# A tile's channel transform made relative to its neighbour's, and half of the four-point step given to GpSimd, in the Fourier layer of an encoder

## The chip, the cores and the metric

The kernel runs on one core of one Trainium2 chip. A core has TensorE (PE; its weight loads are shown apart, as PEld), VectorE (DVE), ScalarE (ACT), GpSimd (POOL) and SyncE (SP), and DMA queues fed by SP, ACT and POOL. The metric is the device time of one execution in microseconds. Of three runs of the kernel before, the median was 1577.85 us (1577.05 to 1578.53).

## The reference

An encoder of width 1024 with two layers is applied to two sequences, one of 2048 positions and one of 512: first windowed attention, then Fourier mixing, each behind an RMS norm, and a last RMS norm. The change is in the Fourier layer:

```python
def fourier_layer(x, g, w_gate, w_out):
    b, s, d = x.shape
    h = rmsnorm(x, g)
    hg = h.astype(jnp.float32).reshape(b, s, N_FGROUPS, FGROUP_CH)
    f = jnp.fft.fftn(hg, axes=(1, 3), norm="ortho").real
    f = f.reshape(b, s, d).astype(x.dtype)
    gate = h @ w_gate
    return x + (f * jax.nn.silu(gate)) @ w_out
```

There are four groups of 256 channels. The two-dimensional transform is a transform over the channels of each group, then one over the positions.

## The kernel before

The attention layer fills the time to about 1058 us, the Fourier layer the rest. This layer's first stage, from about 1060 to 1323 us and called the gates stage here, works on the 20 tiles of 128 positions as ten pairs. The four tiles of the short sequence are one group of four; the long sequence's tiles a, a+4, a+8 and a+12, for a of 0 to 3, are the other four. Two successive pairs are one group; gi is a group's number, n a pair's (0 to 9).

**What a pair goes through.** Its two tiles are loaded, normed (L1056, L110, L111 and the multiplication on L1081), and turned on PE (transposes, L1089). The turned tiles are then combined: F[1] to F[4] are sums and differences of the two tiles' halves (`sums`, an ACT copy on L1112 for some, and DVE on L1119), and `odd` makes one more difference in the bank (L1103). Each matrix that PE is to multiply is held as two parts, a rounded one and what the rounding left: ACT casts, DVE subtracts (`split`, L1013 and L1015; `own`, L1096 and L1097). The parts of F[i] are S[i], those of a turned tile A.

**The gate products** of a pair (`gates`) are six products of 128x512, W, Z and X being their three PSUM banks. Two pairs of tiles share multiplications in a Strassen-like scheme, so that sums of banks give the four blocks of the result: c11, c12, c22 and W itself. DVE adds on L1227 (c12 and Z), L1232 (c22 and W) and L1236 (c11 and X). After L1232 PE writes W again, with the product named N4. Each block goes through a SiLU (tanh on ACT, L1197, a scalar-tensor-tensor on DVE, L1198) into a buffer gt and by POOL's queue to memory (s2d, L1201).

**The channel transform** of the next pair's two tiles is done between these products, at the hooks. Hooks 1 to 4 turn and combine the next pair, hook 5 does its second tile, hook 6 its first:

- The second tile (`z_odd_even`, at hook 5) uses S[1] and the parts of the bank that `odd` made: an even and an odd half, 16 matmuls of 128x256. Each of four banks is taken out by an ACT copy of the odd half with a factor (L1160) and a DVE scalar-tensor-tensor that adds the even half (L1161).
- The first tile (`z`, at hook 6) multiplies its own parts A by both halves of the table in three products each (`matmul3`, L117): 24 matmuls of 128x256. Each of two banks is taken out by one ACT copy (L1139).

The results are 128x1024 buffers, zs[0] and zs[1].

**The four-point step** (`radix4`, called by `combine`, at hook 6 of every second pair) takes the four z of a group: six operations of 128x1024 on DVE (L1261). Four results go to memory by POOL's queue (L1337), except those of the last group (gi = 4), which stay on the chip. The six, with z0 to z3 for the four z:

```python
e = z0+z2; z0 = z0-z2; z2 = z1+z3; z1 = z1-z3; z3 = e-z2; e = e+z2
```

**What sets the order.** Each engine works its own queue in order, which a scheduler makes from the order of the program text; semaphores hold an instruction until what it reads is ready or what it overwrites has been read. Buffers with a fixed number of copies are taken in turn: five PSUM banks for transposes and transforms, three for W, Z and X, eight of the kind hT, sixteen for z and other 128x1024 tiles (R).

Of the kernel before, what the change touches and what calls it, by code (L numbers as in the profile page):

```python
# [10 lines left out]
F32R = mybir.dt.float32r  # L11
# [3 lines left out]
ALU = mybir.AluOpType  # L15
# [4 lines left out]
P = 128  # L20
# [22 lines left out]
def encoder(  # L43
# [3 lines left out]
    PE, ACT, DVE, POOL, SP = nc.tensor, nc.scalar, nc.vector, nc.gpsimd, nc.sync  # L47
# [18 lines left out]
    odd = dram.tile([3, 2, P, D], F32, name="odd")  # L66
# [38 lines left out]
    def htile(shape, dtype, name):  # L105
        return main.tile(shape, dtype, align_bytes=LINE, tag="hT", bufs=8, name=name)
# [884 lines left out]
    def fourier_phase(tail):  # L991
        with ExitStack() as es:
# [10 lines left out]
            def right(shape, dtype, name):  # L1003
                return zp.tile(shape, dtype, align_bytes=LINE, tag="R", bufs=16, name=name)
# [3 lines left out]
            def zt(name):  # L1008
                return right([P, D], F32, name)

            def split(t, src, lo_engine=DVE, place=lambda key, ins: ins):

                place("act", ACT.copy(t[:, 0], src))  # L1013
                for cs in (slice(0, 256), slice(256, 512)) if lo_engine is POOL else (slice(0, 512),):
                    place("dve", lo_engine.tensor_tensor(t[:, 1, cs], src[:, cs], f32(t[:, 0, cs]), ALU.subtract))  # L1015
                return t[:, 0], t[:, 1]
# [51 lines left out]
            class Pair:  # L1068
# [71 lines left out]
                        out, ps.rearrange("p (g o n) -> p g o n", g=2, o=2), AF.Copy, scale=1.0 if t >= SEQ // P else 0.5  # L1140
                    )

                def z_odd_even(self):

                    t = self.ts[1]
                    self.zs[1] = zt(f"z{t}")
                    for g in range(4):
                        ps = bank(f"z{t}_{g}")
                        for odd, m in enumerate((self.S[1], self.diff)):

                            to = ps[:, odd * 256 : odd * 256 + 256].rearrange("p (a n) -> p a n", a=2)
                            for part in range(2):
                                PE.matmul(
                                    to, m[part][:, g * P : (g + 1) * P], ch[:, 0, :, odd * P : (odd + 1) * P],
                                    start=part == 0, stop=part == 1,
                                )
                        v = ps.rearrange("p (o a n) -> p a o n", o=2, a=2)
                        out = self.zs[1][:, g * 256 : g * 256 + 256].rearrange("p (n o) -> p o n", o=2)
                        scale = 1.0 if t >= SEQ // P else 0.5
                        ACT.activation(out, v[:, 1], AF.Copy, scale=scale)  # L1160
                        last_z[0] = DVE.scalar_tensor_tensor(out, v[:, 0], scale, out, ALU.mult, ALU.add)  # L1161
# [98 lines left out]
            def tt(out, a, b, op):  # L1260
                DVE.tensor_tensor(out, a, b, op)  # L1261

            def radix4(z, name):

                e = zt(f"e{name}")
                tt(e, z[0], z[2], ALU.add)
                tt(z[0], z[0], z[2], ALU.subtract)
                tt(z[2], z[1], z[3], ALU.add)
                tt(z[1], z[1], z[3], ALU.subtract)
                tt(z[3], e, z[2], ALU.subtract)  # L1270
                tt(e, e, z[2], ALU.add)
                return e, z[3], z[0], z[1]
# [6 lines left out]
            pairs = [Pair(2 * gi + i // 2, tiles[i : i + 2]) for gi, tiles in enumerate(order) for i in (0, 2)]  # L1279
# [43 lines left out]
            def turns4(pr):  # L1323
                pr.sums(3)
                pr.parts(3)

            def combine(pr):

                if pr.n % 2 == 0:
                    return  # L1330
                gi = pr.n // 2
                r = radix4(pairs[pr.n - 1].zs + pr.zs, f"r{gi}")
                if gi == 4:
                    kept.extend(r)
                    return
                for i in range(4):
                    POOL.dma_start(gsd[i] if gi == 0 else evd[gi - 1, i] if i < 2 else odd[gi - 1, i - 2], r[i])  # L1337
# [3 lines left out]
            pr = pairs[0]  # L1341
# [16 lines left out]
            for n, pr in enumerate(pairs[:-1]):  # L1358
                nx = pairs[n + 1]
                if n:  # L1360
                    for i in range(2):
                        nx.load(1 - i)
                        nx.norms(1 - i)
                gates(pr, {
                    1: [lambda: turns1(nx)], 2: [lambda: turns2(nx)], 3: [lambda: turns3(nx)], 4: [lambda: turns4(nx)],
                    5: [lambda: nx.z_odd_even()],
                    6: [lambda: nx.z(0), lambda: nx.z(1), lambda: combine(nx)],
                })
            gfb = fp.tile([P, D], F32, tag="gb", bufs=1, name="gfb")
            SP.dma_start(gfb, bass.AP(gf.tensor, gf.offset, [[0, P], [1, D]]))  # L1370
# [386 lines left out]
            for i, l in enumerate((w0, w2)):  # L1757
                for a in range(3):
                    t = zt(f"ev{a}_{i}")
# [15 lines left out]
            e, g4r = pm(w0[0], w0[2], "e0")  # L1775
            f, g4s = pm(w0[1], w0[3], "f0")
# [16 lines left out]
            for a in range(4):  # L1793
                for i, l in enumerate((pc, qs)):
# [3 lines left out]
                    t = zt(f"od{a}_{i}")  # L1798
# [28 lines left out]
            o = Outs(6, position("p6", 6, *G[6], pair(6, 16, 0), None, p6))  # L1827
# [19 lines left out]
            for k1, k2 in ((1, 7), (7, 3), (3, 5), (5, None)):  # L1847
                name, tiles = f"p{k1}", pair(k1, 16, 0)
# [29 lines left out]
                o = nxt["o"]  # L1878
# [108 lines left out]
```

## Time and profile before

| | |
|---|---|
| median of three runs | 1577.85 us |
| the profiled execution: its time, its span | 1577.83 us, 1576.1 us |
| PE busy | 1565.2 us, 99% of the span |
| DVE busy | 1150.7 us, 73% |
| ACT busy | 878.1 us, 56% |
| POOL busy | 444.6 us, 28% |
| one pair in the gates stage (pairs 4 to 7) | 25.66 to 25.67 us |

The profile is of one execution. Its busy time counts how long an engine had an instruction under way. A row of a timeline gives the start in us from the span's beginning, the duration, the engine, the line, the operation, what it writes and reads with the shape, and how many such instructions are in the row; in brackets stands how long the engine was idle before it and what ended that. A row of the chain of waits gives a start, a duration and the work that the end of the span depended on. A row of groups gives the number of instructions, their busy time and the mean of one in ns, then the idle time ahead of them. Names such as W, Z, X, z, c and gt are those of the program; tTb and tTd are parts of turned tiles, trb the bank a transpose wrote, invb and ssb the norm's sums.

### The profile page before, as it was taken

Reading aid. Unit: us, or ns where it says so; the run is one execution under the profiler, and the core shown is the slowest. Engines: PE = TensorE matmul, PEld = TensorE weight load, DVE = VectorE, ACT = ScalarE, POOL = GpSimd, SP = SyncE. Lnnn points to the kernel's source line nnn. Section 1 sums busy time; section 2 is a strip of 40 time slices with the busy share of each in tenths; the row PEclk is TensorE's granted clock in tenths of the full one; section 3 lists DMA queues with packets and bytes.
Section 4 is the critical chain, followed back from the end, with each engine's and each line's share of the span. In section 5 each row is a group of like instructions: output and inputs, shape, how many; then the busy total and the mean of one; then the engine's idle time right before and its main releaser. Section 6 shows DMA issues by size and latency. Waiting matters only on the chain.

```text
span 1576.1 us, 27737 instructions
## 1 busy us (share of the span) xinstructions
PE 1565.2 (99%) x9882; PEld 1315.6 (83%) x9882; DVE 1150.7 (73%) x2793; ACT 878.1 (56%) x2096; POOL 444.6 (28%) x614
## 2 busy tenths in 40 slices
PE   9999999999999999999999999999999999999998
PEld 7888888888888888988888888888888888888886
DVE  6888555877548786378764577668878778989886
ACT  7788535776247684257852477646655554333353
POOL 2575642421404314024223242222111111101100
PEclk9999999999999999999999999999999999999999
DMA  8598695565856667656649656675666569557852
GB/s 296 203 332 287 223 365 210 208 247 202 297 214 214 204 248 256 242 193 235 238 170 326 232 208 208 248 253 200 210 222 233 185 219 399 193 201 267 312 195 94
DMA packets 100997, 373.90 MB, mean 237 GB/s; under 512 B 11268, under 2 KB 22284, under 8 KB 83453
## 3 DMA queue, kind: packets, MB, share of 16 engines
q1 hardware_dynamic: 83148, 298.17, 53.7%
q0 software_dynamic: 16400, 70.04, 11.5%
q10 hardware_dynamic: 1312, 3.94, 0.6%
q8 instruction: 78, 1.28, 0.3%
q14 instruction: 59, 0.48, 0.1%
HBM read 280.84 MB, written 91.26 MB: 236 GB/s over the span
## 4 chain that ended last, share of the span: by engine, by line
PE 94%; DVE 4%; issue 1%; ACT 1%; DMA 0%; POOL 0%; SPq 0%; POOLq 0%; DVEq 0%; ACTq 0%
PE gp L117 14%; PE qp L117 14%; PE spt L117 11%; PE op L117 7%; PE W L117 7%; PE av L615 6%; PE spt L530 6%; PE fo L117 5%; PE vp L117 3%; PE Z L117 3%; PE pt L589 3%; PE Wo L117 3%; PE z L117 2%; PE X L117 2%; PE Zo L117 2%; PE ABp L117 1%
## 5 line engine op out<-in xcount | busy, mean ns | idle before, releaser
L117 PE MATMUL gp<-h,wg 128*128 128x512 f32 x960 | 237.7, 396 | 0.0
L117 PE MATMUL qp<-h,wq 128*128 128x512 f32 x960 | 237.0, 396 | 0.0
L549 DVE CUSTOM_DVE_ANT_0 S<-spt,b 128x385 f32<-128x385 f32 (+1 forms) x320 | 156.5, 528 | 105.5 <-PE spt L530 68.3
L117 PEld LDWEIGHTS gp<-h,wg 128*128 128x128 f32 x960 | 174.9, 188 | 37.3 <-issue 1.0
L117 PEld LDWEIGHTS qp<-h,wq 128*128 128x128 f32 x960 | 174.9, 188 | 36.4 <-issue 0.3
L557 ACT ACTIVATE S<-S 128x385 f32<-128x385 f32 (+1 forms) x320 | 188.8, 596 | 19.5 <-DVE S L549 19.3
L597 ACT CAST pts<-pt 128x384 fp32r<-128x384 f32 (+1 forms) x240 | 100.6, 458 | 167.0 <-PE pt L589 158.2
L598 DVE TENSOR_TENSOR pts<-pt,pts 128x384 fp32r<-128x384 f32 (+1 forms) x240 | 114.3, 520 | 23.4 <-ACT pts L597 22.2
L639 POOL TENSOR_TENSOR uT<-o,uT 128x256 fp32r<-128x256 f32 x75 | 55.6, 741 | 229.5 <-ACT uT L638 229.4
L117 PE MATMUL spt<-wo,uT 128*128 128x512 f32 x480 | 120.3, 391 | 0.0
L117 PE MATMUL op<-wo,uT 128*128 128x512 f32 x480 | 118.9, 391 | 0.0
L530 PE MATMUL spt<-kwin,qab 64*128 64x384 f32 (+1 forms) x960 | 118.8, 353 | 0.0
L615 PEld LDWEIGHTS av<-pts,v 128*128 128x128 f32 x576 | 101.4, 188 | 18.8
L615 PE MATMUL av<-pts,v 128*128 128x512 f32 (+1 forms) x576 | 115.7, 341 | 0.0
L117 PE MATMUL fo<-wo,tTu 128*128 128x512 f32 x480 | 115.4, 392 | 0.0
L117 PEld LDWEIGHTS op<-wo,uT 128*128 128x128 f32 x480 | 89.4, 188 | 18.5
L117 PEld LDWEIGHTS spt<-wo,uT 128*128 128x128 f32 x480 | 89.1, 188 | 18.3
L117 PEld LDWEIGHTS fo<-wo,tTu 128*128 128x128 f32 x480 | 88.3, 188 | 17.3
L569 DVE TENSOR_SCALAR S<-S 128x384 f32<-128x384 f32 (+1 forms) x192 | 95.9, 499 | 6.8
L530 PEld LDWEIGHTS spt<-kwin,qab 64*128 64x128 f32 x960 | 74.7, 186 | 28.4 <-issue 26.4
L635 POOL TENSOR_TENSOR o<-o,s 128x256 f32<-128x256 f32 x75 | 55.4, 738 | 134.5 <-DVE o L633 134.1
L589 PEld LDWEIGHTS pt<-ident,S 64*128 64x128 f32 x1328 | 78.3, 138 | 4.2 <-issue 2.1
(331 smaller groups left out, 3173.2 us busy)
## 6 DMA issues: line engine op xcount, KB each, us to landing
wo<-wsd SPq DMA_DIRECT2D x32, 1024.0 KB, 5.0
wq<-wsd SPq DMA_DIRECT2D x31, 1024.0 KB, 7.1
wg<-wsd SPq DMA_DIRECT2D x31, 1024.0 KB, 5.8
x<-x1d SPq DMA_DIRECT2D x40, 512.0 KB, 3.9
b<-b21d SPq DMA_DIRECT2D x40, 512.0 KB, 4.8
b<-rowd SPq DMA_DIRECT2D x40, 384.0 KB, 4.3
xs<-in_x_dram SPq DMA_DIRECT2D x23, 512.0 KB, 7.5
s2d<-gt POOLq DMA_DIRECT2D x40, 256.0 KB, 5.2
```

What stands on the lines that cost most here:

```text
L117: ins = pe(PE.matmul(out, a[i], b[j], start=start and i + j == 0, stop=stop and i == 1, skip_group_check=more))
L530: pe(PE.matmul(banks[j][:, 2 + k0 * P : 2 + k1 * P], res["q"][rows, qp, b * P : (b + 1) * P], kwin[g][rows, kp, b * P + k0 * P : b * P + k ...
L549: seq(DVE, DVE.tensor_tensor_reduce(out=s[:, e0:e1], in0=ps[:, 1 + e0 : 1 + e1], in1=st["bias"][:, j, 386 - e1 : 386 - e0][:, ::-1], scale ...
L557: last_exp[0] = seq(ACT, ACT.activation(s[:, e0:e1], s[:, e0:e1], AF.Exp, bias=s[:, 386:387], scale=-1.0, accum_out=s[:, 387:388]))
L569: seq(DVE, DVE.tensor_scalar(s[:, ks], s[:, ks], den, None, ALU.mult))
L589: pe(PE.transpose(ps[h][:, kb, j, :], ss[j][rows, 1 + kb * P : 1 + (kb + 1) * P], ident[rows, rows]))
L597: seq(ACT, ACT.copy(hi, ps[:, k0:k1]))
L598: seq(DVE, DVE.tensor_tensor(lo, ps[:, k0:k1], f32(hi), ALU.subtract))
L615: pe(PE.matmul(to, v, pt, start=n == part == 0, stop=part == 1 and n in (1, len(todo) - 1), skip_group_check=n > 1,))
L635: eng.tensor_tensor(o, o, s, ALU.mult)
L639: low = eng.tensor_tensor(lo, o, f32(hi), ALU.subtract)
```

## The change

For the pairs with n of 2 or more, the first tile's transform becomes one of the same kind as the second's. `cross`, run at hook 4, replaces F[4] by 2 F[3] - F[4] (one DVE operation) and splits it into a new hT buffer (tC). At hook 6 `z_odd_even(0)` multiplies S[4] and these parts: 16 matmuls for 24, four ACT copies and four DVE operations of 128x256 for two ACT copies of 128x512. Its zs[0] holds the first tile's transform less the second's.

`radix4_relative` then takes the four-point step from such relative inputs, for gi of 1 to 4. It has six operations too. For gi of 1, 2 and 3 three of them (`slow`) go to POOL, each in four pieces of 128x256; for gi = 4 all stay on DVE. The group gi = 0 keeps the old step.

```diff
--- before.py
+++ after.py
@@ -1140,13 +1140,20 @@
                         out, ps.rearrange("p (g o n) -> p g o n", g=2, o=2), AF.Copy, scale=1.0 if t >= SEQ // P else 0.5
                     )

-                def z_odd_even(self):
-
-                    t = self.ts[1]
-                    self.zs[1] = zt(f"z{t}")
+                def cross(self):
+
+                    F3, F4 = self.F[3], self.F[4]
+                    DVE.scalar_tensor_tensor(F4, F3, 2.0, F4, ALU.mult, ALU.subtract)
+                    self.mixed = split(htile([P, 2, 512], F32R, f"tC{self.n}"), F4)
+
+                def z_odd_even(self, i=1):
+
+                    t = self.ts[i]
+                    out_of = (self.S[1], self.diff) if i else (self.S[4], self.mixed)
+                    self.zs[i] = zt(f"z{t}")
                     for g in range(4):
                         ps = bank(f"z{t}_{g}")
-                        for odd, m in enumerate((self.S[1], self.diff)):
+                        for odd, m in enumerate(out_of):

                             to = ps[:, odd * 256 : odd * 256 + 256].rearrange("p (a n) -> p a n", a=2)
                             for part in range(2):
@@ -1155,7 +1162,7 @@
                                     start=part == 0, stop=part == 1,
                                 )
                         v = ps.rearrange("p (o a n) -> p a o n", o=2, a=2)
-                        out = self.zs[1][:, g * 256 : g * 256 + 256].rearrange("p (n o) -> p o n", o=2)
+                        out = self.zs[i][:, g * 256 : g * 256 + 256].rearrange("p (n o) -> p o n", o=2)
                         scale = 1.0 if t >= SEQ // P else 0.5
                         ACT.activation(out, v[:, 1], AF.Copy, scale=scale)
                         last_z[0] = DVE.scalar_tensor_tensor(out, v[:, 0], scale, out, ALU.mult, ALU.add)
@@ -1260,6 +1267,22 @@
             def tt(out, a, b, op):
                 DVE.tensor_tensor(out, a, b, op)

+            def on_pool(out, a, b, op):
+                for i in range(4):
+                    cs = slice(i * 256, i * 256 + 256)
+                    POOL.tensor_tensor(out[:, cs], a[:, cs], b[:, cs], op)
+
+            def radix4_relative(z, name, slow=tt):
+
+                e = zt(f"e{name}")
+                tt(e, z[0], z[2], ALU.add)
+                slow(z[0], z[0], z[2], ALU.subtract)
+                tt(z[2], z[1], z[3], ALU.add)
+                slow(z[1], z[1], z[3], ALU.subtract)
+                DVE.scalar_tensor_tensor(z[2], z[2], 2.0, e, ALU.mult, ALU.add)
+                slow(z[0], z[0], z[1], ALU.add)
+                return z[2], e, z[0], z[1]
+
             def radix4(z, name):

                 e = zt(f"e{name}")
@@ -1323,13 +1346,19 @@
             def turns4(pr):
                 pr.sums(3)
                 pr.parts(3)
+                if pr.n > 1:
+                    pr.cross()

             def combine(pr):

                 if pr.n % 2 == 0:
                     return
                 gi = pr.n // 2
-                r = radix4(pairs[pr.n - 1].zs + pr.zs, f"r{gi}")
+                zs = pairs[pr.n - 1].zs + pr.zs
+                if gi:
+                    r = radix4_relative(zs, f"r{gi}", tt if gi == 4 else on_pool)
+                else:
+                    r = radix4(zs, f"r{gi}")
                 if gi == 4:
                     kept.extend(r)
                     return
@@ -1364,7 +1393,7 @@
                 gates(pr, {
                     1: [lambda: turns1(nx)], 2: [lambda: turns2(nx)], 3: [lambda: turns3(nx)], 4: [lambda: turns4(nx)],
                     5: [lambda: nx.z_odd_even()],
-                    6: [lambda: nx.z(0), lambda: nx.z(1), lambda: combine(nx)],
+                    6: [lambda: nx.z_odd_even(0) if nx.n > 1 else [nx.z(hf) for hf in range(2)], lambda: combine(nx)],
                 })
             gfb = fp.tile([P, D], F32, tag="gb", bufs=1, name="gfb")
             SP.dma_start(gfb, bass.AP(gf.tensor, gf.offset, [[0, P], [1, D]]))
```

Ahead of each part below stands the engine and the place. er is e, and a name's first number tells which tile it belongs to.

DVE at the four-point step of gi = 1, made before and during the products of pair 3. Before (z0 and z4 are zs[0] and zs[1] of the group's first pair, z8 and z12 those of its second; afterwards z0 and z8 are the relative ones):

```order
L1081 SCALAR_TENSOR_TENSOR x1_1_13651<-x1_1_13651,invb1_13656,g1b_12526 128x1024
L1261 TENSOR_TENSOR er1_13631<-z0_13354,z8_13602 128x1024
L1261 TENSOR_TENSOR z0_13354<-z0_13354,z8_13602 128x1024
L1261 TENSOR_TENSOR z8_13602<-z4_13309,z12_13557 128x1024
L1261 TENSOR_TENSOR z4_13309<-z4_13309,z12_13557 128x1024
L1261 TENSOR_TENSOR z12_13557<-er1_13631,z8_13602 128x1024
L1261 TENSOR_TENSOR er1_13631<-er1_13631,z8_13602 128x1024
L1097 TENSOR_TENSOR tTb5_1_13705<-trb5_1_13700,tTb5_1_13705 128x512
L1119 TENSOR_TENSOR s1_4_13708<-s1_4_13708,trb5_1_13700 128x512
```

After:

```order
L1168 SCALAR_TENSOR_TENSOR z8_13610<-z8_2_13625,z8_13610 128x2x128
L1168 SCALAR_TENSOR_TENSOR z8_13610<-z8_3_13632,z8_13610 128x2x128
L1081 SCALAR_TENSOR_TENSOR x1_5_13659<-x1_5_13659,invb5_13664,g1b_12526 128x1024
L1268 TENSOR_TENSOR er1_13639<-z0_13358,z8_13610 128x1024
L1081 SCALAR_TENSOR_TENSOR x1_1_13668<-x1_1_13668,invb1_13673,g1b_12526 128x1024
L1268 TENSOR_TENSOR z8_13610<-z4_13313,z12_13565 128x1024
L1282 SCALAR_TENSOR_TENSOR z8_13610<-z8_13610,er1_13639 128x1024
L1097 TENSOR_TENSOR tTb5_1_13722<-trb5_1_13717,tTb5_1_13722 128x512
L1119 TENSOR_TENSOR s1_4_13725<-s1_4_13725,trb5_1_13717 128x512
```

The six operations in a row have become three, with the two norm multiplications (L1081) now behind the evacuations and around the first of them; the next pair's first row (tTb) follows the scalar-tensor-tensor.

DVE further on in the same pair, around the addition of c and W. Before:

```order
L1227 TENSOR_TENSOR c12_3_13727<-c12_3_13727,Z3_13661 128x512
L1015 TENSOR_TENSOR S4_4_13776<-s4_4_13749,S4_4_13776 128x512
L1119 TENSOR_TENSOR s4_4_13749<-trb1_0_13729,s4_4_13749 128x512
L1198 SCALAR_TENSOR_TENSOR gt8_1_13772<-gt8_1_13772,c12_3_13727 128x512
L1232 TENSOR_TENSOR c3_13663<-c3_13663,W3_13660 128x512
L1015 TENSOR_TENSOR S3_4_13803<-s4_4_13749,S3_4_13803 128x512
```

After:

```order
L1234 TENSOR_TENSOR c12_3_13744<-c12_3_13744,Z3_13678 128x512
L1015 TENSOR_TENSOR S4_4_13793<-s4_4_13766,S4_4_13793 128x512
L1119 TENSOR_TENSOR s4_4_13766<-trb1_0_13746,s4_4_13766 128x512
L1205 SCALAR_TENSOR_TENSOR gt8_1_13789<-gt8_1_13789,c12_3_13744 128x512
L1146 SCALAR_TENSOR_TENSOR s4_4_13766<-s4_4_13766 128x512
L1239 TENSOR_TENSOR c3_13680<-c3_13680,W3_13677 128x512
L1015 TENSOR_TENSOR S3_4_13820<-s4_4_13766,S3_4_13820 128x512
L1015 TENSOR_TENSOR tC4_13824<-s4_4_13766,tC4_13824 128x512
```

The crossing (L1146 of the new text) stands between the SiLU of c12 and the addition of c and W; the new split (tC) stands behind that addition and S[3].

POOL over the same place. Before:

```order
L1201 DMA s2d0_81<-gt4_0_13598 128x512
L1337 DMA odd_83<-z0_13354 128x1024
L1337 DMA odd_83<-z4_13309 128x1024
L1337 DMA evd_113<-z12_13557 128x1024
L1337 DMA evd_113<-er1_13631 128x1024
L1201 DMA s2d0_81<-gt8_1_13772 128x512
```

After:

```order
L111 TENSOR_TENSOR invb1_13673<-invb1_13673,mhalf_77 128x1
L1273 TENSOR_TENSOR z0_13358<-z0_13358,z8_13610 128x256 x4
L1366 DMA evd_113<-er1_13639 128x1024
L1273 TENSOR_TENSOR z4_13313<-z4_13313,z12_13565 128x256 x4
L1273 TENSOR_TENSOR z0_13358<-z0_13358,z4_13313 128x256 x4
L1366 DMA evd_113<-z8_13610 128x1024
L1366 DMA odd_83<-z0_13358 128x1024
L1366 DMA odd_83<-z4_13313 128x1024
L1208 DMA s2d0_81<-gt8_1_13789 128x512
```

Three groups of four pieces now stand among the four stores, all ahead of the next gated tile's store.

## The prediction

> **What bounds the kernel now.** I read the page's totals first, then its chain, then the stage the change touches: the busy time of each engine in four successive pairs of the gates stage.
>
> ```profile
> span 1576.1 us, 27737 instructions
> PE 1565.2 (99%) x9882; PEld 1315.6 (83%) x9882; DVE 1150.7 (73%) x2793; ACT 878.1 (56%) x2096; POOL 444.6 (28%) x614
> PEclk9999999999999999999999999999999999999999
> PE 94%; DVE 4%; issue 1%; ACT 1%; DMA 0%; POOL 0%; SPq 0%; POOLq 0%; DVEq 0%; ACTq 0%
> ```
> ```profile
> 1169.52:1195.19 25.67, 25.67 (x143) 22.22 (x142) 17.05 (x29) 13.99 (x27) 4.03 (x8) 1.00 0.44 163
> 1195.19:1220.85 25.66, 25.66 (x142) 22.21 (x141) 23.31 (x34) 13.99 (x27) 4.88 (x9) 1.00 0.75 259
> 1220.85:1246.52 25.67, 25.67 (x142) 22.22 (x141) 17.36 (x30) 14.14 (x27) 4.22 (x8) 1.00 0.42 152
> ```
>
> The columns of the second fence are the stretch, its length, then PE, PEld, DVE, ACT and POOL busy, the clock and DMA. PE is busy the whole 25.67 us of every pair, at full clock (the PEclk row, and 1.00 here). So a matmul taken away shortens the pair by its own time, as long as everything else still arrives. DVE is the next engine: 17 us in a pair without a four-point step, 23.31 of 25.66 in one with it. ACT at 14 and POOL at 4 to 5 have room. Everything below is about whether DVE, given more small work, still delivers to PE in the pairs with a four-point step.
>
> **The change part by part.** *Matmuls removed.* The chain of waits between 1165 and 1225 us shows both channel transforms and what stands around them:
>
> ```profile
> 1187.82 1.91 PE z L1153 x16
> ...
> 1210.08 2.72 PE W L117 x12
> 1212.80 0.68 PE X L117 x3
> 1213.48 1.91 PE z L1153 x16
> 1215.40 2.75 PE W L117 x12
> 1218.14 2.87 PE z L117 x24
> ```
>
> The first tile's transform, 24 matmuls of 128x256 in 2.87 us, becomes 16 of the kind that now take 1.91 us for the second tile. That is 0.96 us for each of the eight pairs with n of 2 to 9: 8 x 0.96 = **-7.68 us**. No cover is needed, since PE is the bound.
>
> *DVE and ACT work added.* The mean duration of each kind of instruction in the gates stage:
>
> ```profile
> L1015 DVE TENSOR_TENSOR S<-s,S 128x512 fp32r<-128x512 f32 x40 | 27.5, 688 | 0.2
> L1013 ACT CAST S<-s 128x512 fp32r<-128x512 f32 x40 | 24.9, 623 | 32.9 <-DVE s L1119 18.1 <-PE W L117 12.2 <-PE Z L117 2.5
> L1081 DVE SCALAR_TENSOR_TENSOR x<-x,invb,g1b 128x1024 f32<-128x1024 f32 x16 | 20.5, 1279 | 8.9 <-POOL invb L111 8.9
> L1261 DVE TENSOR_TENSOR z<-z,z 128x1024 f32<-128x1024 f32 x15 | 18.4, 1225 | 0.4
> L1161 DVE SCALAR_TENSOR_TENSOR z<-z,z 128x256 f32<-128x256 f32 x40 | 14.4, 415 | 0.0
> L1139 ACT ACTIVATE z<-z 128x512 f32<-128x512 f32 x20 | 12.6, 632 | 8.3 <-PE z L117 8.2
> L1160 ACT ACTIVATE z<-z 128x256 f32<-128x256 f32 x40 | 12.6, 393 | 0.8 <-PE z L1153 0.8
> ```
>
> Per changed pair DVE gets the crossing (one 128x512 of the L1015 size, 0.69), the low half of its split (0.69) and four evacuations (4 x 0.415 = 1.66): 3.04 us. ACT gets a cast (0.62) and 4 x 0.393 for 2 x 0.632: +0.93, hidden at 14 of 25.67. In pairs without a four-point step DVE goes from 17 to 20 of 24.7 us, and it sits idle for long stretches there, ahead of the next tiles' work:
>
> ```profile
> 1224.91 1.28 DVE L1081 SCALAR_TENSOR_TENSOR x<-x,invb,g1b 128x1024 f32<-128x1024 f32 x1 [4.01 <-POOL invb L111]
> 1228.70 0.69 DVE L1097 TENSOR_TENSOR tTb<-trb,tTb 128x512 fp32r<-128x512 f32 x1 [2.50 <-ACT tTb L1096]
> ```
>
> So I cost the added work there at nothing; the cover is these 4.01 and 2.50 us. For the group of gi = 4 all six operations stay on DVE (one as a scalar-tensor-tensor of the same size), and no next pair's transposes stand behind them: nothing again.
>
> *The four-point step with pieces on GpSimd (gi = 1, 2, 3).* Three 128x1024 operations leave DVE, 3 x 1.225 = 3.68 us; twelve pieces of 128x256 come to POOL. POOL's rows for pieces of that shape, and a DVE row beside the second of them:
>
> ```profile
> 1072.63 1.43 POOL L1015 TENSOR_TENSOR wN<-w32N,wN 128x256 fp32r<-128x256 f32 x2 [12.36 <-ACT wN L1013]
> 1076.09 1.89 POOL L1015 TENSOR_TENSOR wN<-w32N,wN 128x256 fp32r<-128x256 f32 x2 [2.03 <-ACT wN L1013]
> ```
> ```profile
> 1077.30 1.23 DVE L1015 TENSOR_TENSOR wT<-w32N,wT 128x512 fp32r<-128x512 f32 x1
> ```
>
> Two pieces take 1.43 us alone, so four take 2.9, and twelve 8.7: in POOL's free 20 us, but not in parallel with DVE at will. The second pair of pieces took 1.89, +0.46, and the DVE operation between two SBUF operands beside them took 1.23 where its kind takes 0.69 (the S row): +0.54. The two hold each other up. [...]
>
> Where DVE stands in such a pair today, from 1195.19 us on (t = 0, where PE begins a pair's first product):
>
> ```profile
> 1191.66 0.41 DVE L1161 SCALAR_TENSOR_TENSOR z<-z,z 128x256 f32<-128x256 f32 x1
> ...
> 1196.06 1.23 DVE L1261 TENSOR_TENSOR er<-z,z 128x1024 f32<-128x1024 f32 x1
> 1197.32 3.75 DVE L1261 TENSOR_TENSOR z<-z,z 128x1024 f32<-128x1024 f32 x3
> ...
> 1202.35 1.22 DVE L1261 TENSOR_TENSOR er<-er,z 128x1024 f32<-128x1024 f32 x1
> 1203.50 0.69 DVE L1097 TENSOR_TENSOR tTb<-trb,tTb 128x512 fp32r<-128x512 f32 x1
> ...
> 1205.46 0.69 DVE L1015 TENSOR_TENSOR S<-s,S 128x512 fp32r<-128x512 f32 x1
> ...
> 1211.23 0.68 DVE L1119 TENSOR_TENSOR s<-trb,s 128x512 f32<-128x512 f32 x1
> 1211.83 0.68 DVE L1198 SCALAR_TENSOR_TENSOR gt<-gt,c 128x512 f32<-128x512 f32 x1
> 1212.84 0.69 DVE L1232 TENSOR_TENSOR c<-c,W 128x512 f32<-128x512 f32 x1 [0.33 <-PE W L117]
> ```
>
> The four-point step ends, and the next tiles' work (tTb) begins, at 1203.50, t = 8.3. The addition that reads PE's bank W (c and W, L1232) ends at 1213.53. PE overwrites W in the products that the chain shows from 1215.40, t = 20.2: 1.87 us of slack. In the changed order this piles up: the first tile's evacuations now follow its last matmul (t = 0) through ACT and DVE. One takes at least 0.393 + 0.415 = 0.8 us; the second tile's last one ended 2.3 us after its last matmul (1191.66 + 0.41 against 1187.82 + 1.91), since both engines had other work. I take 1.8; then the first norm's multiplication (1.28, now behind them) to 3.0, the first sum (1.23) to 4.15, the second norm's multiplication to 5.35. POOL's four pieces of z0-z2 may begin at 4.15, but that multiplication reads two SBUF operands and holds them to 5.35: they end at 5.35 + 2.9 = 8.25. Only then may DVE overwrite z2 (1.23, to 9.5), then the scalar-tensor-tensor (1.23): tTb begins at t = 10.7, 2.4 us later than now. What took three more DVE operations takes less DVE time and ends later, because DVE waits for POOL. From there to c and W the row of work is as before without its 0.33 us wait, plus the crossing, which now stands ahead of it (0.60, the distance of two such rows: 1211.23 to 1211.83). It ends at 18.34 - 0.33 + 2.4 + 0.6 = 21.0, against 20.2: PE stalls 0.8. If one of the operations between SBUF operands on the way (S at 1205.46, say) meets POOL's remaining eight pieces, 0.54 more: 1.35. I take **1.0 us**, between them, three times: +3.0. Bounds: 0 (next part) and the slower rival's.
>
> *Smaller terms.* The two transforms now need eight bank fills among five banks, and the third of the first tile's waits for the second tile's evacuation, which stands behind the late c and W: between 0 and one evacuation (0.415), I take 0.25, three times: +0.75. In the first changed pair (n = 2, prepared beside the old four-point step with all of its six operations) the crossing likewise delays c and W and the new split; that pair has no POOL pieces, so 0 to 1.0, middle 0.5, once. POOL's stores of the four results start later; the next stores of gated tiles come at t near 20, when POOL's pieces (from 9.5 on, 8 x 0.74, to about 15.5, with two stores to 17) are over: nothing.
>
> **Sum:** -7.68 + 3.0 + 0.75 + 0.5 = -3.4 us. The profiled execution took 1577.83 us, 1.7 beyond its span, and the median of the runs is 1577.85: the same. Predicted 1574.4 us. A measurement here tells about 0.2% from no change, 3.2 us: the bounds are 1574.7 and 1581.0.
>
> **The rivals.** *All of the gain stays.* If POOL's first pieces run beside the norm's multiplication without waiting (4.15 to 7.1), tTb begins at 9.6 and c and W ends at 19.9, ahead of 20.2: no stall. Then only the small terms are left, 0 to 1.25: 1570.2 to 1571.4. For it: most DVE operations there read PSUM and, like tTb, have one SBUF operand, and the first wN row shows no lengthening. Against it: the 1.23 us row.
>
> *The gain is eaten.* Two or three more of the operations between SBUF operands collide, 0.54 each, so the stall is 1.6 to 3.2 a pair: 1576.2 to 1581. For it: POOL has pieces waiting over some 6 to 7 us of that stretch.
>
> *Slower.* DVE and POOL alternate: every DVE operation between SBUF operands from the scalar-tensor-tensor to c and W (that one, three S, gt, the crossing: six) waits out a piece, 6 x 0.54 = 3.2, and POOL's first pieces take another 0.5 as in the second wN row. That is 0.8 + 3.7 = 4.5 a pair: -7.68 + 13.5 + 1.25 = +7.1, 1584.9. It decides from (7.68 + 3.16 - 1.25) / 3 = 3.2 us a pair. For it: +0.54 is what the row at 1077.30 shows of a meeting. Against it: 12 pieces are 8.7 us, and 4 of them lie ahead of the tTb row, so there aren't pieces enough for the late ones (gt, crossing) unless POOL itself is held up. [...]
>
> **How the numbers follow.** The forecast (stall 0.6 to 1.6, 1573.2 to 1576.2): 0.42. All of the gain: 0.20. Eaten: 0.20. Slower: 0.18. Faster by over 0.2% is all of the second and some six tenths of the first, 0.46; within 0.2% the rest of the first and the third, 0.36; slower 0.18. The range goes from the full gain, 1570.0, to 1582.0, which leaves out most of the slower case and little else.
>
> **What would show it.** Right: pairs of 24.7 us where there is no four-point step, some 25.9 where its pieces run on POOL; in these PE idle before the products after the second tile's transform, put down to c and W; DVE idle about 2.5 us before z2's overwriting, put down to POOL; POOL pieces above 0.74 us only beside DVE operations between SBUF operands. Wrong: PE idle in pairs without a four-point step (the added DVE work has no cover), PE waiting for the new split rather than for c and W, or pieces above 1 us throughout.

## The result

The changed kernel is slower. In four runs it took 1587.74 us (median; 1586.05 to 1588.49), the kernel before 1578.19 us (four runs, 1577.05 to 1578.56). The ratio is 1.0059, with a 95% interval of 1.0047 to 1.0072: +9.5 us where -3.4 was forecast, and outside the range given (1570 to 1582).

The page of the profile after, whose execution took 1586.05 us, has the same shape as before, and PE's busy time has fallen by less than the removed matmuls should give:

```profile
span 1584.3 us, 27730 instructions
PE 1563.5 (99%) x9818; PEld 1310.6 (83%) x9818; DVE 1159.9 (73%) x2832; ACT 882.9 (56%) x2120; POOL 476.1 (30%) x650
```

The pairs 3 to 7, each from PE's first product to that of the next, with the columns as in the prediction, tell where it went:

```profile
1143.17:1171.37 28.20, 25.48 (x135) 21.42 (x133) 22.06 (x36) 14.44 (x32) 15.97 (x22) 1.00 0.61 218
1171.37:1196.07 24.70, 24.70 (x134) 21.25 (x133) 19.44 (x36) 14.21 (x31) 3.67 (x8) 1.00 0.49 159
1196.07:1226.39 30.32, 26.70 (x134) 22.63 (x133) 22.88 (x40) 15.38 (x34) 16.18 (x22) 0.94 0.66 232
1226.39:1252.62 26.23, 26.23 (x133) 22.39 (x133) 18.81 (x33) 13.78 (x27) 3.49 (x7) 0.94 0.39 148
1252.62:1280.27 27.65, 25.45 (x134) 21.41 (x133) 22.06 (x36) 14.29 (x31) 15.98 (x22) 1.00 0.62 222
```

The pair of 24.70 us is the forecast's: 25.66 less 0.96, with nothing lost. The three pairs with pieces on GpSimd (POOL busy for 16 us) take 28.20, 30.32 and 27.65, and the one of 26.23 follows the longest with a clock below 1.00. Above 24.70 that is 3.50 + 5.62 + 1.53 + 2.95 = 13.6 us, which eats the 7.68 and 5.9 more. With 1.6 us lost in the first changed pair, 1.2 behind the pairs and 0.4 won ahead of them, that is the span's 8.2 us to 0.1. The list of waits from 1143 to 1305 us has, for the matmuls themselves, these two rows (total, times, longest):

```profile
PE z L1160 <- DVE z L1168: 7.4, 5, 3.1
...
PE W L117 <- DVE c L1239: 1.2, 3, 0.6
```

The second row is the forecast's wait, for the addition of c and W: 1.2 us in all, where it said 3.0. The first was not forecast at this size. PE waits to begin a bank of the first tile's transform, since an evacuation of the second tile's banks isn't done. In the longest of these pairs the timelines of SP, POOL, ACT, DVE and PE (taken engine by engine) show what stood behind it:

```profile
1213.26 5.11 SPq L1076 DMA_DIRECT2D x<-x1d  x2
```
```profile
1212.57 0.57 POOL L1366 DMA_DIRECT2D evd<-z  x1
1213.13 1.06 POOL L1366 DMA_DIRECT2D odd<-z  x2
```
```profile
1220.61 1.06 ACT L1056 ACTIVATE jkb<-x 128x1024 bf16<-128x1024 f32 x1 [3.77 <-DMA x<-x1d]
...
1221.66 0.61 ACT L1204 ACTIVATE gt<-c 128x512 f32<-128x512 f32 x1
1222.18 0.66 ACT L1167 ACTIVATE z<-z 128x256 f32<-128x256 f32 x2
```
```profile
1206.57 0.68 DVE L1097 TENSOR_TENSOR tTb<-trb,tTb 128x512 fp32r<-128x512 f32 x1
...
1212.51 0.68 DVE L1015 TENSOR_TENSOR S<-s,S 128x512 fp32r<-128x512 f32 x1
...
1216.11 0.68 DVE L1239 TENSOR_TENSOR c<-c,W 128x512 f32<-128x512 f32 x1
```
```profile
1223.39 0.79 PE L1160 MATMUL z<-chan_sb,S 128*128 128x256 f32 x2 [3.06 <-DVE z L1168]
```

The load of a tile of the pair after next (x, L1076) overwrites the buffer that DVE's S at 1212.51 reads, so it begins at 1213.26, t = 17.2 of the pair, where it began at 15.0 before (1210.19 less 1195.19). The three late stores of the four-point step are given to the DMA engines between 1212.57 and 1214.19, around it. The load lands at 1220.6, after 7.3 us. ACT's queue has this tile's squares (L1056, for the norm) ahead of the second tile's evacuations, which have long been ready. ACT stands for 3.77 us, and DVE, which adds to what ACT has copied, with it. PE has filled the fifth bank and has no other: it idles 3.06 us.

The timelines of before, of SP and POOL in the same pair, show the same load free of this:

```profile
1210.19 4.35 SPq L1076 DMA_DIRECT2D x<-x1d  x2
```
```profile
1203.87 0.54 POOL L1337 DMA_DIRECT2D evd<-er  x1 [0.72 <-DVE er L1261]
```

There the last store was given away 6 us ahead of the load, which took 4.5 us up to the squares.

### The profile page after: what moved, and what is told of

The parts are those of the page before. It is cut to its first block, busy times and chain, and to the rows that moved or that the text cites. A ratio compares the mean times of both kernels' runs of the same rounds, so it can differ in the third digit from the quotient of the medians.

```text
span 1584.3 us, 27730 instructions
## 1 busy us (share of the span) xinstructions
PE 1563.5 (99%) x9818; PEld 1310.6 (83%) x9818; DVE 1159.9 (73%) x2832; ACT 882.9 (56%) x2120; POOL 476.1 (30%) x650
## 3 DMA queue, kind: packets, MB, share of 16 engines
q0 software_dynamic: 16400, 70.04, 11.4%
q8 instruction: 78, 1.28, 0.3%
## 5 line engine op out<-in xcount | busy, mean ns | idle before, releaser
L557 ACT ACTIVATE S<-S 128x385 f32<-128x385 f32 (+1 forms) x320 | 188.8, 596 | 19.5 <-DVE S L549 19.3
L117 PEld LDWEIGHTS spt<-wo,uT 128*128 128x128 f32 x480 | 89.1, 188 | 18.3
```

The lines of the kernel that those rows point to most:

```text
L117: ins = pe(PE.matmul(out, a[i], b[j], start=start and i + j == 0, stop=stop and i == 1, skip_group_check=more))
L557: last_exp[0] = seq(ACT, ACT.activation(s[:, e0:e1], s[:, e0:e1], AF.Exp, bias=s[:, 386:387], scale=-1.0, accum_out=s[:, 387:388]))
```

## The experiments

Two theories were set against each other. A: the late stores make the load late, and the load holds up ACT's queue. B: eight evacuations among five banks are too many, whatever the load does. A third, that pieces on GpSimd cost by themselves, came in with the second group of runs. Times are medians of the runs, ratios are to the kernel before with a 95% interval. "A pair" is one with a four-point step of gi = 1, 2 or 3.

### The channel transform alone

```diff
-                    r = radix4_relative(zs, f"r{gi}", tt if gi == 4 else on_pool)
+                    r = radix4_relative(zs, f"r{gi}")
```

> The channel transform as changed, but all six operations of every four-point step on DVE. Theory A (a late load): in the changed kernel the load of a tile (x, L1076) starts 2.2 us later in a pair with pieces on GpSimd, takes 7.3 us instead of 3.7 because the four results are stored at the same time, and ACT, which works in order, stands at that tile's squares (L1056) ahead of the evacuations of the second tile's banks; PE then has no bank. Here the results are stored while DVE still computes, so the load takes some 4 us: no idle PE at the first tile's transform, but 1.5 to 2 us of PE waiting for the addition of c and W in each of the three pairs, as DVE's row gets longer: 1576 to 1580 us. Theory B (too few banks for the eight evacuations, whatever the load does): PE still idles 2 to 3 us a pair at the first tile's transform: 1584 to 1588 us.

1574.99 us (1573.09 to 1576.91); ratio 0.9979 (0.997 to 0.9989). The channel transform's change is worth its evacuations. The time is on A's side, a little below the 1576 to 1580 expected, and far from B's 1584 to 1588. In its list of waits for the stretch of the pairs there is none for c and W, and of those for a bank's evacuation none either; what is left is

```profile
PE trb L1089 <- DVE x L1081: 0.6, 1, 0.6
PE z L1160 <- ACT tC L1013: 0.5, 2, 0.3
```

So with six operations on DVE, DVE isn't later for c and W than PE allows: the 1.5 to 2 us expected there did not come. The first load of x starts as late as in the changed kernel (t = 17.4) and took 3.7 to 4.4 us in the three pairs. There are the same eight evacuations and five banks, and no wait for them, which speaks against B. But one thing more differs than was meant. The scheduler set ACT's row in another order here, with the second tile's four evacuations ahead of the squares:

```profile
1160.84 0.89 ACT L1167 ACTIVATE z<-z 128x256 f32<-128x256 f32 x2 [0.22 <-PE z L1160]
...
1162.13 0.67 ACT L1167 ACTIVATE z<-z 128x256 f32<-128x256 f32 x2
...
1163.80 1.06 ACT L1056 ACTIVATE jkb<-x 128x1024 bf16<-128x1024 f32 x1 [0.50 <-DMA x<-x1d]
```

So this run alone doesn't tell the load's time from ACT's order; the runs with the late stores and on the kernel before do, below. This kernel is faster than the one before and the changed one. It doesn't get the whole 7.68: PE's last pair began 5.7 us earlier than before (1292.14 for 1297.85), but the span shrank by 3.4 (1572.7 for 1576.1). The chain that follows that pair has a load of output weights in it:

```profile
1317.84 12.77 DMA w32f<-in_w_fout_dram
```

It was issued 25.7 us into the pair, as before (1323.54 less 1297.85), and PE then waited for it. From 5 to 8 us into that pair on the DMA engines are fully busy (a share of 1.01 to 1.09 for 35 us and more) in the kernels before, after and this one, so it is likely that time won ahead of this stretch is partly lost in it; that wasn't tested.

### GpSimd's part alone

```diff
-                    6: [lambda: nx.z_odd_even(0) if nx.n > 1 else [nx.z(hf) for hf in range(2)], lambda: combine(nx)],
+                    6: [lambda: nx.z(0), lambda: nx.z(1), lambda: combine(nx)],
...
+            def radix4(z, name, slow=tt):
...
-                tt(z[3], e, z[2], ALU.subtract)
+                slow(z[3], e, z[2], ALU.subtract)
                 tt(e, e, z[2], ALU.add)
```

> The channel transforms as before, and three operations of the four-point step (z0-z2, z1-z3, e-z2) on GpSimd in four pieces each for gi = 1, 2, 3. Theory A: the stores are late as in the changed kernel, so a load of x still takes over 5 us in these pairs, but the first tile's transform needs two banks instead of four, so PE waits little: 1577 to 1581 us. Theory B: no added evacuations, no idle PE: 1577 to 1578.5 us. The forecast's mechanism (DVE late for the addition of c and W) gives nothing here, since the crossing is away and DVE's row is no longer than before.

1586.0 us (1585.57 to 1586.34); ratio 1.0054 (1.0037 to 1.007). This run had a fault of its own, which the expectation overlooked: the last sum overwrites e, which GpSimd's last four pieces read, so DVE waits for all twelve pieces:

```profile
1155.03 1.23 DVE L1268 TENSOR_TENSOR er<-er,z 128x1024 f32<-128x1024 f32 x1 [5.71 <-POOL z L1273]
```

The addition of c and W is then late and PE idles 1.56 to 1.59 us for it a pair, with more in front of it. It says what a wait of DVE for GpSimd can cost (2.9 us a pair), not what the change cost. The next run has the sum in a buffer of its own:

```diff
+                f = zt(f"f{name}")
+                tt(f, e, z[2], ALU.add)
+                slow(e, e, z[2], ALU.subtract)
+                return f, e, z[0], z[1]
...
```

> As the run with GpSimd's part alone, with a buffer of its own for the last sum, so that DVE waits for GpSimd's first four pieces only, as in the changed kernel. The channel transforms are as before. By DVE's rows the next tiles' work begins at t = 7.6 of such a pair (8.3 before), so no wait for c and W; the load of x starts near 14.3 and is stretched to some 7 us by the stores, and the first tile's transform needs two banks only: 1577 to 1580 us. If pieces on GpSimd cost by themselves (they hold up every DVE operation between SBUF operands): 1582 us or more.

1589.48 us (1585.83 to 1592.71); ratio 1.0069 (1.0052 to 1.0086). More than either number expected, and by theory A's way, not the other: DVE's operations beside the pieces keep their durations, but for one S a pair of 0.94 or 0.95 us for 0.69, and no wait for c and W shows; the list of waits of one pair has

```profile
ACT jkb L1056 <- DMA x<-x1d: 6.2, 1, 6.2
...
PE z L117 <- DVE z L1168: 3.4, 1, 3.4
```

The load took 9.5 us there. Two banks for the first tile aren't few enough to escape, which the expectation had thought. So the gain is the channel transform's and the loss is that of the step's part on GpSimd: -2.9 us alone against +11.4 alone.

### The stores, moved

First ahead of the pieces, all four sending e (`first` issues them):

```diff
                 tt(e, z[0], z[2], ALU.add)
+                if first:
+                    first(e)
                 slow(z[0], z[0], z[2], ALU.subtract)
...
```

> The changed kernel, but for gi = 1, 2, 3 all four stores of a group send the first sum e, ahead of GpSimd's pieces: the same bytes leave 10 us earlier, and what they hold isn't the four-point step's results (the position stage then works on those). Theory A: the load of x takes about 4 us again and lands near t = 21 of the pair instead of 24.5; PE's idle time at the first tile's transform (2.4, 3.1 and 1.9 us) and the lowered clock after it go: 1574 to 1578 us. Theory B, or if the late start of the load alone is enough: 1584 us or more.

1576.85 us (1575.31 to 1578.63); ratio 0.9995 (0.9985 to 1.0005): 11 us less than the changed kernel with the same work on all engines. The load starts as late as there (t = 17.4) and takes 4.0, 5.5 and 4.5 us in the three pairs. PE's waits that are left are for the new split (2.0 us in all), whose cast stands on ACT behind the squares. Here too the scheduler set the second tile's four evacuations ahead of the squares on ACT, so that two things changed at once. The next run has the stores behind the first load of x, with the true results (`anchor` is the pair's last store of a gated tile):

```diff
-                for i in range(4):
-                    POOL.dma_start(gsd[i] if gi == 0 else evd[gi - 1, i] if i < 2 else odd[gi - 1, i - 2], r[i])
+                def put(anchor=None):
+                    for i in range(4):
+                        after(POOL.dma_start(gsd[i] if gi == 0 else evd[gi - 1, i] if i < 2 else odd[gi - 1, i - 2], r[i]), anchor)
...
-                    6: [lambda: nx.z_odd_even(0) if nx.n > 1 else [nx.z(hf) for hf in range(2)], lambda: combine(nx)],
+                    6: [lambda: held.pop()(last_s[0]) if held else None, lambda: nx.z_odd_even(0) if nx.n > 1 else [nx.z(hf) for hf in range(2)], lambda: combine(nx)],
```

> The changed kernel with its pieces on GpSimd and its true results, the four stores of gi = 1, 2, 3 held back behind the pair's last store of a gated tile, some 8 us later, so that they leave after the first load of x. The order on DVE and ACT is that of the changed kernel. Theory A (the stores stretch the load, the load holds up ACT's row): the first load of x in these pairs takes some 4 us again, PE's idle time at the first tile's transform falls from 1.9 to 3.1 us to under 1 a pair: 1574 to 1580 us, the upper end if the stores then stretch the second load or hold z's buffers. If the later start of the load alone is the cause: 1584 us or more.

1577.63 us (1575.59 to 1578.03); ratio 0.9993 (0.9983 to 1.0002). In this layer PE, DVE and ACT have the changed kernel's order to the row, so the stores are all that moved. The first load takes 3.5 to 4.7 us, and PE's waits over all the pairs are

```profile
PE W L117 <- DVE c L1239: 0.9, 3, 0.3
PE z L1160 <- DVE z L1168: 0.8, 2, 0.4
```

7.4 us of waiting for evacuations have become 0.8; c and W still cost 0.9. The eight evacuations, the five banks and the order are those of the changed kernel, so B falls. The late start of the load (t = 16.9 here), which both kernels keep, is by itself nearly free. But the two kernels are 1.9 and 2.6 us slower than the one with all six operations on DVE (1574.99), a difference that their intervals barely tell apart. So no gain of GpSimd's part shows even with the stores out of the way; where the 2 us go was not followed.

### The squares, moved

The stores and the load stay as they are; ACT may not take the squares ahead of the second tile's last evacuation:

```diff
-                    inv = sumsq(xt, f"b{self.ts[i]}")
+                    inv = sumsq(xt, f"b{self.ts[i]}", lambda key, ins: after(ins, last_za[0]) if key == "act" else None)
...
```

> The changed kernel, with one ordering added: ACT's squares of a norm (L1056) may not be issued ahead of the last evacuation of the second tile's banks. Loads and stores stay as late as in the changed kernel. Theory A: PE's idle time at the first tile's transform goes although the load still takes 7 us: 1574 to 1578 us. Theory B: it stays, 1584 us or more. If the late tile itself were the bound, the idle time would move to the next pair's transposes (L1089): 1582 us or more.

1580.25 us (1577.8 to 1581.96); ratio 1.0015 (1.0006 to 1.0025). The first load takes 6.0 to 7.6 us still, and the wait for evacuations is gone:

```profile
PE W L117 <- DVE c L1241: 1.5, 3, 0.7
PE trb L1089 <- DVE x L1081: 0.9, 3, 0.4
```

The idle time at the next pair's transposes, foreseen as the late tile's own price, is 0.9 us in all. It is 2 us above the number expected; the pairs account for some of it, the stretch behind them (274.95 us from the last pair's first product to PE's end, 272.61 in the changed kernel) for the rest. With the stores moved the loss goes, and with the squares moved 7.5 us of it, so both links of A are shown: the stores stretch the load (5.7 to 7.3 us, 3.5 to 4.7 with the stores moved), and that counts because its squares stand ahead in ACT's queue.

### One store or four ahead of the load

The last three runs take the kernel before, with every row of PE, DVE and ACT in its place, and only hold back its four stores of a pair by a tiny GpSimd operation that reads something of the next pair: F[4] in the first run, as here, F[2] in the second, the split of the odd difference in the third:

```diff
+                if held:
+                    t = fp.tile([P, 8], F32, tag="tick", bufs=1, name=f"tick{pr.n}")
+                    s = pr.F[4]
+                    held.pop()(POOL.tensor_tensor(t[:, :1], s[:, :1], mhalf[:, :1], ALU.pow))
...
```

> The kernel before, unchanged on PE, DVE and ACT, with the four stores of gi = 1, 2, 3 held back by a tiny GpSimd operation that reads F[4] of the next pair, so that they leave at about t = 15 of the pair with the first load of x, instead of 4 to 9. No pieces on GpSimd, no crossing, no added evacuations. Theory A (late stores alone do it): the load takes 7 us or more, ACT stands at the squares, PE idles 1 to 3 us at the first tile's transform of these pairs, with the clock lowered where that is over 2.4 us: 1581 to 1589 us. If the pieces on GpSimd or DVE's lateness are needed for it: 1577 to 1579 us.

> As the run with the late stores on the kernel before, where the first store left 0.35 us after the load and the load still took 3.9 us; here GpSimd's tiny operation reads F[2] instead, so that about two of the four stores leave ahead of the load of x, as in the changed kernel, with nothing else changed. Theory A', sharpened (a store that is issued ahead of the load makes the load late, one issued behind it doesn't): the first load takes 5 to 7.5 us, PE idles up to 1.5 us a pair, 1578.5 to 1583 us. If the order of store and load doesn't matter: 1578 to 1579 us, load near 4 us.

> The same with the tiny operation reading the split of the odd difference, so that all four stores leave in the 2 us ahead of the load of x. Theory A': the load takes 7 to 10 us, ACT stands at the squares for 3 to 6 us, PE idles 1 to 3.5 us at the first tile's transform, with the clock lowered after the longest: 1581 to 1590 us. If the pieces on GpSimd are needed for it: 1578 to 1579 us.

Medians: 1578.44 us (ratio 1.0002, 0.9992 to 1.0011), 1578.69 us (1.0005, 0.9995 to 1.0014) and 1584.09 us (1.0047, 1.0026 to 1.0067). In the first the stores came 0.35 us behind the load, and the first load was on time; it was the pair's second that took 8 us, at little cost. The first expectation falls, and with it the plain form of A. In the second two stores were ahead and the third's issue had begun 0.15 to 0.19 us before the load; the load took 5.9 to 6.3 us, and PE idled 0.3 us in two pairs, too little to show in the time. In the third all four were ahead; its timeline of SP and ACT and its waits, for one pair:

```profile
1158.01 4.39 SPq L1076 DMA_DIRECT2D x<-x1d  x2
```
```profile
1167.14 1.06 ACT L1056 ACTIVATE jkb<-x 128x1024 bf16<-128x1024 f32 x1 [5.81 <-DMA x<-x1d]
```
```profile
PE z L117 <- DVE z L1161: 3.1, 1, 3.1
```

The load took 9.1, 7.9 and 7.6 us in the three pairs, and PE idled 3.10, 1.89 and 1.52. The order of PE, DVE and ACT in this layer is that of the kernel before: +6 us by the time at which four stores leave. The changed kernel, with one store ahead of its load and two issued around the load's start, has 6.3, 7.3 and 5.7 us and 2.4, 3.1 and 1.9 us of idle PE.

One number orders all of these pairs: when ACT begins the squares, counted from the pair's start. In the runs with two and four stores ahead and in the one with the sum in its own buffer, PE's idle time at the first tile's transform is what this start lies beyond t = 21.0, to 0.01 us: 0.30 for 21.30, 1.52 for 22.52, 3.10 for 24.09, 3.43 for 24.43. In the changed kernel 22.69, 23.23 and 24.54 gave 1.90, 2.42 and 3.06, what lies beyond 20.8 to 21.5. So it makes little difference whether two banks are to be filled or four, and B has no part in it. It also shows how two delays add up. Before, the squares begin at 18.3 to 19.5, with 1.5 to 2.7 us to spare. The changed kernel's load starts 1.9 to 2.2 us later, which uses most or all of that up, and what the stores add to the load's time is then paid in full. Without the late start, loads of 5.9 to 6.3 us cost 0.34 us at most; without the stretch, in the run with the late stores, the late start cost 0.85 us in one pair.

### A part kept, and a run on the clock

Here `last` is GpSimd's pieces for gi = 1, 2 and 3, and the two other operations are DVE's:

```diff
-                slow(z[0], z[0], z[1], ALU.add)
+                last(z[0], z[0], z[1], ALU.add)
...
```

> The changed kernel, with only the last of the three (z0+z1, for which DVE never waits) on GpSimd for gi = 1, 2, 3, the other two on DVE. Beside the run with all six on DVE (1574.99 us): one DVE operation of 1.23 us less in these pairs, four pieces on GpSimd beside DVE's operations, and one store 2 us later. Theory A: 1573 to 1576 us. If pieces on GpSimd cost by themselves: 1577 us or more.

1576.16 us (1574.79 to 1578.26); ratio 0.9988 (0.9979 to 0.9997). Four pieces for which nobody waits, beside DVE's operations, do no harm that can be told from the run with none (1574.99), and no good.

```diff
+                for k in range({2: 4, 4: 6, 6: 8, 8: 10}.get(n, 0)):
+                    held[0] = after(DVE.tensor_tensor(c22, c22, c22, ALU.max), held[0]) or held[0]
                 last_c[0] = DVE.tensor_tensor(c22, c22, W, ALU.add)
...
```

> The kernel before, with 4, 6, 8 and 10 DVE operations of 128x512 (the larger of c22 and itself, which changes nothing) ahead of the addition of c and W in the pairs 2, 4, 6 and 8, so that PE idles there for some 1, 2, 3 and 4 us once each. If a longer idle time lowers PE's clock, as the row of 3.06 us in the changed kernel suggests, the granted clock falls to 0.5 for some 6 us after idle times of 3 us and more and not after those under 2; the time is 1577.9 plus the idle times plus some 3 us for each such fall: about 1594 us. If the clock fell there for another reason: 1588 us, with the clock at 1.00 throughout.

1583.89 us, one run. It did not test what it should: the order around the added operations moved too, the first tile's transform came into the gap, and only the last of the four waits became an idle PE, of 2.37 us. Behind that one the clock was low, at 0.56 and 0.87 in the two stretches of 3 us that follow.

## Why the prediction was wrong

*What held.* The matmuls: 0.96 us a pair, shown by 24.70 for 25.66. The added DVE and ACT work in pairs without a four-point step: hidden, as said. DVE's wait for GpSimd's first pieces: 2.72 us, about 2.5 forecast, with tTb at t = 10.5 for 10.7 and c and W ending at 20.7 for 21.0. That the norm's multiplication holds up these pieces was an estimate from the wN rows. In the longest pair of the changed kernel the first of them began 0.22 us behind that multiplication (1.28 us) and took 1.65 us, the next three 0.73 each, and the four ended at t = 8.07 for 8.25. The wait of PE for c and W is real and is the one forecast, but 0.3, 0.56 and 0.30 us and not 1.0.

*What failed.* The step that failed is a sentence among the smaller terms: "POOL's stores of the results start later" and what followed from it, "nothing". It looked at the next stores in POOL's queue and not at who shares the DMA engines at the new time: their busy share was 0.97 over the load's 7.3 us, and 0.62 over its 4.5 us in the kernel before. Three of the four stores went from t = 4 to 9 to t = 16.5 to 18, and the load of x from 15.0 to 17.2. Nor did the prediction follow the load itself, though its own sum moved the row that frees its buffer by 2.4 us; and behind the load stands ACT's queue. The term for the banks (0.25 a pair, bounded by one evacuation) named the right place, the wait of the first tile's transform for the second tile's evacuations, and put the wrong thing ahead of it, the late addition of c and W. It measured 1.9 to 3.1 us a pair, and with the lowered clock these pairs and the one behind the longest lost 12.4 us beside c and W (13.6 less 1.2), for 0.75 forecast. It was the second of the first tile's four banks that waited, not the third. The first changed pair lost 1.6 us (the two pairs around it took 50.6 for 49.0) where 0.5 was said; 1.07 of it is PE's wait, at the next transposes, for the multiplication on L1081. The stretch behind the pairs lost 1.2 us, which wasn't forecast.

*The rivals.* "Slower" had a size close to this (+7.1), but not its mechanism: DVE and GpSimd were to alternate at every operation between SBUF operands. In the changed kernel the rows beside the pieces show DVE's 128x512 operations at 0.68 to 0.70 us throughout. It was POOL's pieces that were held up:

```profile
1200.39 3.75 POOL L1273 TENSOR_TENSOR z<-z,z 128x256 f32<-128x256 f32 x4 [2.96 <-PE X L117]
...
1205.54 7.09 POOL L1273 TENSOR_TENSOR z<-z,z 128x256 f32<-128x256 f32 x8 [0.87 <-issue]
```

That is 0.9 us more than alone in the first four (2.9) and 1.3 more in the eight that follow (5.8). Three of the twelve pieces took longer, 1.65, 1.71 and 1.22 us for 0.73 to 0.75. They had begun 0.22, 0.12 and 0.08 us behind DVE operations between SBUF operands (L1081, L1282, L1015) and ended 0.6 us behind them. DVE paid where the piece came first. In the run with the last four pieces alone, one began 0.12 us ahead of S:

```profile
1154.36 1.16 DVE L1015 TENSOR_TENSOR S<-s,S 128x512 fp32r<-128x512 f32 x1
```

So a meeting cost DVE 0.48 us, near the rival's 0.54, but there was one a pair and not six, and that run shows no loss in time. In these rows, then, DVE lost nothing where its operation began first, and 0.48 us where the piece did. The cost of one meeting was sized about right, their number was not; the loss lay in the DMA traffic.

## What to carry to other kernels

When a change moves work in time, its stores move with it (here three of four by some 10 us): look in the trace for what else uses the DMA engines at the new time, and for the engine on whose queue the wait for that transfer stands ahead of work that others need. A load that is waited for in an in-order queue is on the path of everything behind it, also where its own reader has time: here ACT's 3.77 us at the squares became 3.06 us of idle PE. And when two edits come as one, as here a worthwhile transform with a costly placement, cost and try each by itself.

## What the runs showed of the hardware

**In these runs a load's time went by the stores given away ahead of it.** A load of 512 KB took 3.9 us with the four stores (512 KB each) issued from 0.35 us behind it, 5.9 to 6.3 with two ahead and a third just begun, 7.6 to 9.1 with four ahead. The stores were not all that counted: with no such store near, but another load of 512 KB (b) issued 0.55 us ahead in the same queue, it took 5.5 (early stores, second pair), and with two such loads and three stores begun in the 1.5 us ahead 8.5 to 9.5 (the sum in its own buffer).

**The clock.** Towards the end of the 3.06 us of idle PE (1220.33 to 1223.39), at 1222.86, the granted clock fell to 0.50, and 6.83 us later it was back at 1.00. The windows of the changed kernel:

```profile
1218.00:1222.00 4.00, 2.33 (x13) 1.80 (x11) 0.58 (x1) 1.39 (x3) 0.00 (x0) 1.00 1.00 392
1222.00:1224.00 2.00, 0.61 (x3) 0.61 (x4) 1.65 (x4) 2.00 (x7) 0.55 (x1) 0.71 1.07 342
1224.00:1228.00 4.00, 4.00 (x15) 3.51 (x15) 3.72 (x12) 2.67 (x7) 1.10 (x2) 0.50 0.90 286
1228.00:1230.00 2.00, 2.00 (x7) 1.53 (x7) 0.84 (x2) 0.00 (x0) 1.17 (x2) 0.58 1.03 418
1230.00:1232.00 2.00, 2.00 (x10) 1.67 (x9) 1.13 (x1) 0.59 (x1) 0.00 (x0) 1.00 0.48 195
```

Some 2.8 us were lost that way beside the idle time. PE's busy time is 2.0 us longer in that pair, but also 0.75 to 0.78 longer in the two others with pieces, at full clock; the remaining 1.2 and the 1.53 of the next pair go with the clock. The length of an idle time alone did not tell whether it happened: it did after 2.37, 2.57, 3.06 and 3.43 us, and not after 1.48, 2.00, 2.40 and 3.10. The traces show more. Within each, the changes of the granted clock lie whole multiples of 3.41 us apart: 6.83 in the changed kernel, 3.42, 51.20 and 3.40 with the sum in its own buffer, 3.42 in the run on the clock. Cut into stretches of 3.41 us that end at a change, each of the four falls came at the end of a stretch in which PE was idle for 2.33 to 2.54 us. The 2.40 us that did nothing (the sum in its own buffer, third pair) lay across two stretches, 1.35 and 1.04 us in each, and the 2.00 us of the changed kernel likewise, 1.07 and 0.93, with 0.42 more in the second. How the 3.10 us lay (four stores ahead) was not shown. So where both could be read, the idle time inside one stretch told the falls from the others; where between 1.35 and 2.33 us the bound lies stays open.
